# Hybrid retention and short-convolution block: seven-product groups with 512-wide matmuls, 40 input groups in that form, retention after them, and part sums made by an accumulating DMA

## Chip, cores and metric

One Trainium2 chip, one of its NeuronCores. The metric is the device time of one execution in microseconds (us), the median of several runs. Engines are named as in the profile: PE (matrix multiply), PEld (its weight loads), DVE (vector), ACT (scalar activation), POOL (which also issues DMAs), SP (which issues the weight loads from memory).

## What is computed

One encoder layer on 512 tokens of width 2048, in float32:

```python
h = rmsnorm(x, norm_gain)
proj = h @ w_in                       # 2048 x 12288
q, k, v, g_ret, c_b, c_c, c_x, g_conv, merge_logits = split(proj)
o = bidirectional_retention(rotary(q), rotary(k) * 128 ** -0.5, v)   # 8 heads of 128
branch_ret = o * rsqrt(mean(o * o) + EPS) * ret_gn_gain * silu(g_ret)
branch_conv = c_b * conv3(c_c * c_x) * silu(g_conv)
up = [branch_ret @ w_branch[0], branch_conv @ w_branch[1]]           # each 1024 x 2048
merged = sum(sigmoid(merge_logits) * up)
x = rmsnorm(x + merged @ w_out, final_gain)                          # 2048 x 2048
```

## The kernel before

Every float32 operand is split into a high and a low part in the PE's own format (`split_to`: ACT writes the high part, L140, DVE the remainder, L141). A product of two operands takes three matmuls (`mm3`, L145 to L147): high by high, high by low and low by high, all accumulated in one region of PSUM.

The work is a list of *pieces*, each of four k-tiles (128 rows) by 256 columns of a weight matrix. `run` keeps the loads of weights (SP's queue, L105, three buffers) three pieces ahead, the splits two ahead (three buffers for the high part, two for the low), calls the piece's matmuls, and then pops one entry of the list `background`. An order is only proposed in this way: a scheduler at build time fixes the order on each engine by its own estimates. On the chip each engine runs its instructions in that order and waits where an input is late. A DMA that POOL issues waits in POOL's queue for its inputs in the same way.

The input projection has 48 groups of 256 columns, four pieces each: 4 for each of q, k, v and the retention gate g, 16 for the convolution branch, 16 for the merge gates.

- `group` (L171) makes the eight 128-column by 512-token products of a piece (96 matmuls of 512 columns in a group). `group_tok` (L277, for v) puts tokens on the output's partitions: 192 matmuls of 256 columns.
- `group_s` (L197) replaces eight products of half blocks by seven, in the manner of Strassen and Winograd: the 2 x 2 blocks are two k-tiles by two column halves, and two k-tiles by two token halves of 256. Seven combinations of weight blocks (three of them summed on DVE in `sums`, L134 to L136) meet seven combinations of token blocks (`token_forms`, L263: sums and differences of h, made once per pair of k-tiles and kept in SBUF). `combine` (L247) adds the seven results with one copy on ACT (L253) and four additions on DVE (L255 to L260), reading PSUM. 27 groups go this way: 16 of the convolution, 11 of the merge gates.

Order: transposes of x and the first k group; for each of four pairs of heads the groups k, q, v, g, with the retention of that pair (`retention_steps`, L528: eight steps for two heads: decay table, scores, output, norm, store to memory by POOL) popped from `background` one step per piece; three plain gate groups, under which the token forms are made; the 27 seven-product groups; two plain gate groups, during which both branches are loaded back and split; the two up-projections, alternating by column group; the output projection with the final norm. Results that are needed later (gates, branch outputs) go to memory and come back by POOL's queue.

## Time and profile before

| | us |
|---|---|
| median of 3 runs | 1443.73 (1442.91 to 1446.1) |
| the profiled execution | 1444.66 |
| its span in the trace | 1442.8 |
| granted PE clock, mean | 0.995 of full speed |

The span runs from the first to the last event of the trace; the execution's own time has a little beside it. Busy time of PE is a union of overlapping records, so the price of a matmul is read from the distance between starts. "Idle before, releaser" says what ended an engine's wait. An engine off the limiting chain may be idle at no cost.

### The profile page before, as it was taken

How to read it: one execution, taken by the hardware profiler on the slowest of the kernel's cores; microseconds unless marked ns; L12 is line 12 of the kernel's file. 1: busy time of each engine (PE TensorE's matmuls, PEld its weight loads, DVE VectorE, ACT ScalarE, POOL GpSimd, SP SyncE). 2: the span in 40 equal slices, each digit the busy share in tenths (PEclk: the TensorE clock that was granted, in tenths of full speed). 3: DMA queues.
4: the chain of work that ended last, by engine and by line, in shares of the span. 5: the costliest groups of instructions: out<-in, count | busy, mean ns of one | idle time of the engine just before them, and what ended most of it. 6: DMA issues, size and time to landing. Idle time of an engine off the chain costs nothing.

```text
span 1442.8 us, 20988 instructions
## 1 busy us (share of the span) xinstructions
PE 1423.4 (99%) x8810; PEld 1286.1 (89%) x8810; DVE 945.2 (66%) x1220; ACT 549.2 (38%) x586; POOL 65.8 (5%) x80
## 2 busy tenths in 40 slices
PE   8999999999999999999999999999999999999997
PEld 7888988988988899999999999999978888888886
DVE  4846557466467989988898899889643444522433
ACT  6435335354344434443344334434342222222421
POOL 0000000000000000000000000000010000201210
PEclk9999999999999999999999999999999999999999
DMA  6322322322323333443344334433464444543412
GB/s 229 94 87 84 107 77 86 102 79 97 102 68 121 117 95 106 140 132 103 103 132 135 100 116 134 132 103 103 148 231 161 146 146 146 186 179 102 162 55 105
DMA packets 140610, 174.93 MB, mean 121 GB/s; under 512 B 5940, under 2 KB 122724, under 8 KB 139876
## 3 DMA queue, kind: packets, MB, share of 16 engines
q1 hardware_dynamic: 132788, 143.17, 30.7%
q0 software_dynamic: 7696, 30.41, 6.3%
q8 instruction: 69, 1.13, 0.3%
q14 instruction: 25, 0.20, 0.0%
q10 hardware_dynamic: 32, 0.01, 0.0%
HBM read 156.79 MB, written 16.78 MB: 120 GB/s over the span
## 4 chain that ended last, share of the span: by engine, by line
PE 92%; DVE 5%; DMA 2%; issue 1%; ACT 0%; SPq 0%; DVEq 0%; ACTq 0%
PE acc L147 29%; PE acc L145 29%; PE acc L146 29%; DVE wlo L141 2%; DMA raw<-in_w_in_dram 1%; PE op L147 1%; PE sp L147 1%; PE sp L145 1%; PE op L145 1%; PE op L146 1%; PE sp L146 1%; DVE raw L134 0%; PE xtp L346 0%; DMA xb<-in_x_dram 0%; DVE fl L141 0%
## 5 line engine op out<-in xcount | busy, mean ns | idle before, releaser
L141 DVE TENSOR_TENSOR wlo<-raw,whi 128x1024 fp32r<-128x1024 f32 (+2 forms) x257 | 402.5, 1568 | 351.0 <-PE acc L147 139.8
L140 ACT ACTIVATE whi<-raw 128x1024 fp32r<-128x1024 f32 (+2 forms) x257 | 339.6, 1326 | 560.1 <-PE acc L146 312.9
L147 PE MATMUL acc<-hTh,wlo 128*128 128x256 f32 (+1 forms) x1192 | 396.0, 332 | 2.4 <-DVE wlo L141 2.4
L145 PE MATMUL acc<-hTh,whi 128*128 128x256 f32 (+1 forms) x1192 | 396.6, 333 | 0.7 <-DVE de L257 0.7
L146 PE MATMUL acc<-hTl,whi 128*128 128x256 f32 (+1 forms) x1192 | 395.9, 332 | 0.0
L147 PEld LDWEIGHTS acc<-hTh,wlo 128*128 128x128 f32 x1192 | 227.0, 190 | 24.9 <-DVE wlo L141 3.3
L147 PE MATMUL acc<-fh,wlo 128*128 128x256 f32 x864 | 245.5, 284 | 2.6 <-DVE wlo L141 2.6
L145 PEld LDWEIGHTS acc<-hTh,whi 128*128 128x128 f32 x1192 | 227.2, 191 | 22.1 <-issue 0.8
L146 PEld LDWEIGHTS acc<-hTl,whi 128*128 128x128 f32 x1192 | 227.1, 191 | 21.2
L145 PE MATMUL acc<-fh,whi 128*128 128x256 f32 x864 | 244.6, 283 | 0.3 <-DVE T L574 0.2
L146 PE MATMUL acc<-fl,whi 128*128 128x256 f32 x864 | 244.5, 283 | 0.0
L147 PEld LDWEIGHTS acc<-fh,wlo 128*128 128x128 f32 x864 | 166.1, 192 | 3.6 <-DVE wlo L141 3.3
L145 PEld LDWEIGHTS acc<-fh,whi 128*128 128x128 f32 x864 | 166.0, 192 | 0.8 <-DVE T L574 0.4
L146 PEld LDWEIGHTS acc<-fl,whi 128*128 128x128 f32 x864 | 166.0, 192 | 0.0
L146 PE MATMUL acc<-wlo,mTh 128*128 128x512 f32 (+1 forms) x272 | 102.5, 377 | 0.0
L147 PE MATMUL acc<-whi,mTl 128*128 128x512 f32 (+1 forms) x272 | 102.5, 377 | 0.0
L145 PE MATMUL acc<-whi,mTh 128*128 128x512 f32 (+1 forms) x272 | 102.5, 377 | 0.0
L145 PE MATMUL acc<-bh,whi 128*128 128x512 f32 x256 | 99.6, 389 | 0.0
L146 PE MATMUL acc<-bl,whi 128*128 128x512 f32 x256 | 99.6, 389 | 0.0
L147 PE MATMUL acc<-bh,wlo 128*128 128x512 f32 x256 | 99.6, 389 | 0.0
L134 DVE TENSOR_TENSOR raw<-raw 128x512 f32<-128x512 f32 x108 | 74.3, 688 | 16.4 <-DMA raw<-in_w_in_dram 16.3
L146 PE MATMUL acc<-wlo,hTh 128*128 128x256 f32 x256 | 72.4, 283 | 0.0
(171 smaller groups left out, 1546.0 us busy)
## 6 DMA issues: line engine op xcount, KB each, us to landing
raw<-in_w_in_dram SPq DMA_DIRECT2D x191, 512.0 KB, 3.6
raw<-in_w_branch_dram SPq DMA_DIRECT2D x32, 512.0 KB, 3.3
raw<-in_w_out_dram SPq DMA_DIRECT2D x32, 512.0 KB, 3.6
gate_d<-T POOLq DMA_DIRECT2D x16, 512.0 KB, 3.8
gl<-gate_d POOLq DMA_DIRECT2D x16, 512.0 KB, 4.4
y<-in_x_dram POOLq DMA_DIRECT2D x4, 1024.0 KB, 6.6
xb<-in_x_dram SPq DMA_DIRECT2D x12, 256.0 KB, 6.4
ret_d<-tmp POOLq DMA_DIRECT2D x8, 256.0 KB, 2.4
```

Source lines behind the costliest of these rows:

```text
L134: nc.vector.tensor_tensor(s[:, 0:2].rearrange("p f r x -> p r f x"), diag, b21, op=ALU.add)
L140: pin(nc.scalar.activation(hi, src, AF.Copy))
L141: pin(nc.vector.tensor_tensor(lo, src, hi.bitcast(F32), op=ALU.subtract))
L145: pin(nc.tensor.matmul(acc, lh, rh, start=start, stop=False, **kw))
L146: pin(nc.tensor.matmul(acc, lh, rl, start=False, stop=False, **kw))
L147: pin(nc.tensor.matmul(acc, ll, rh, start=False, stop=stop, **kw))
```

## The change

1. In `group_s` the high weight now meets both token parts in one 512-wide matmul, into both halves of a PSUM bank; the low weight meets the high token part in a 256-wide matmul, added into the second half. Seven tiles of one bank each (eight in the pool) replace four banks by two pools. Blocks pair k-tile j with k-tile j + 8.
2. ACT copies each product from PSUM to one SBUF buffer `ev` (one slot) in the group's last piece. `sum_parts` then adds the second halves to the first by an accumulating DMA on POOL's queue, and by a second one adds the product named m1 to two of the sums. `combine` makes the remaining three additions on DVE from SBUF.
3. 40 groups use this form: q, g, all 16 gates and the 16 of the convolution. k (4) and v (4) stay plain. h lies in three tiles, so that for half of the k-tiles a k matmul is cut in two of 256 columns. The token forms are made in the background of the k and the first two v groups.
4. Rotated k and q, v and g go to memory. Retention runs as 22 background entries under the conv up-projection and the last two v groups, from operands that POOL loads back and that are split again; then the ret up-projection follows by itself. A quarter of h is written to memory and read back for those v groups.
5. Pools are re-laid: weights get new buffers after the seven-product stage, in the space of the token forms.

The diff, cut to its core:

```diff
+    big = ctx.enter_context(tc.tile_pool(name="big", bufs=1))
+    tpp = ctx.enter_context(tc.tile_pool(name="tp", bufs=3, reuse_waits="tile"))
...
+        nc.vector.tensor_tensor(s[:, 0:2].rearrange("p f r x -> p r f x"), diag, both21, op=ALU.add)
+        nc.vector.tensor_tensor(b21, s[:, 1], b22, op=ALU.add)
+        nc.vector.tensor_tensor(s[:, 2], b21, b12, op=ALU.add)
...
-                        mm3(
-                            st["acc"][:, j, :],
-                            (wh[:, k, c], wl[:, k, c]),
-                            (rhs()[0][:, kt, :], rhs()[1][:, kt, :]),
-                            kt == 0,
-                            kt == nk - 1,
-                        )
+                        for t, r in rhs(kt):
+                            mm3(
+                                st["acc"][:, j, t : t + r.shape[2]],
+                                (wh[:, k, c], wl[:, k, c]),
+                                (r[:, 0], r[:, 1]),
+                                kt == 0,
+                                kt == nk - 1,
+                                skip_group_check=True,
+                            )
...
-                    pool = ps if state["banks"] % 2 == 0 else fin["psS"]
+                    tiles = [fin["p7"].tile([P, 2, 256], F32, name="acc", tag="acc") for _ in order]
+                    st["acc"] = tiles if state["banks"] else [tiles[i] for i in (4, 5, 6, 2, 3, 0, 1)]
                     state["banks"] += 1
-                    st["acc"] = [pool.tile([P, 2, S], F32, name="acc", tag="acc") for _ in range(2)]
-                for n, (bank, half, b, a) in enumerate(order):
-                    acc = st["acc"][bank // 2][:, bank % 2, half * 256 : half * 256 + 256]
+                for n, (b, a, place) in enumerate(order):
+                    acc = st["acc"][n]
                     for r in range(2):
-                        mm3(
-                            acc,
-                            [weight_form(w, b, r) for w in pc["w"]],
-                            token_form(a, 2 * q + r),
-                            q == 0 and r == 0 and n in seen,
-                            q == KT // 4 - 1 and r == 1,
-                            skip_group_check=True,
-                        )
+                        wh, wl = [weight_form(w, b, r) for w in pc["w"]]
+                        x = token_form(a, q + 4 * r)
+                        first, last = q == 0 and r == 0, q == KT // 4 - 1 and r == 1
+                        nc.tensor.matmul(acc, wh, x, start=first, stop=False, skip_group_check=True)
+                        nc.tensor.matmul(acc[:, 1, :], wl, x[:, 0], start=False, stop=last, skip_group_check=True)
+                    if q == KT // 4 - 1:
+                        nc.scalar.activation(EV()[:, :, place, :], acc, AF.Copy)
                 if q == KT // 4 - 1:
-                    post(combine(*st["acc"]))
-            pieces.append({"dims": (4, 256), "src": src[:, 4 * q : 4 * q + 4, :], "use": use, "forms": True})
+                    sum_parts()
+                    if pc.get("defer"):
+                        state["defer"] = lambda: post(combine())
+                    else:
+                        post(combine())
+            rows = src.rearrange("p (i q) c -> p i q c", q=4)[:, :, q, :]
+            pieces.append({"dims": (4, 256), "src": rows, "use": use, "forms": True})
+
+    def EV():
+
+        return fin["ev"]
+
+    def sum_parts():
+        e = EV()
+        nc.gpsimd.dma_start(out=e[:, 0, 0:7, :], in_=e[:, 1, 0:7, :], accum_op=ALU.add)
+        m1 = e[:, 0, 6:7, :].broadcast_to([P, 2, 256])
+        nc.gpsimd.dma_start(out=e[:, 0, 4:6, :], in_=m1, accum_op=ALU.add)
...
-    def combine(x, y):
-
-        tp = part["tp"]
-        t = tp.tile([P, 2, S], F32, name="T", tag="T", bufs=3)
...
+    def combine():
+
+        e = EV()[:, 0]
+        t = T()
         flat = t.rearrange("p j (i s) -> p (j i) s", i=2)
-        s = tp.tile([P, S], F32, name="sc", tag="sc", bufs=1)
-        nc.scalar.activation(s, x[:, 0, :], AF.Copy)
-        halves = lambda v: v.rearrange("p (i s) -> p i s", i=2)
-        nc.vector.tensor_tensor(flat[:, 1:3, :], halves(s), halves(x[:, 1, :]), op=ALU.add)
-        d = tp.tile([P, S], F32, name="de", tag="de", bufs=1)
-        nc.vector.tensor_tensor(halves(d), halves(s), swapped(x[:, 1, :]), op=ALU.subtract)
-        m1 = y[:, 0, 0:256].unsqueeze(1).broadcast_to([P, 2, 256])
-        nc.vector.tensor_tensor(halves(d), halves(d), m1, op=ALU.add)
-        nc.vector.tensor_tensor(flat[:, 0:4:3, :], halves(d), halves(y[:, 1, :]), op=ALU.add)
+        s, back = e[:, 0:2, :], e[:, 3, :]
+        back = bass.AP(back.tensor, back.offset, [back.ap[0], [-256, 2], [1, 256]])
+        nc.vector.tensor_tensor(flat[:, 1:3, :], s, e[:, 2:4, :], op=ALU.add)
+        nc.vector.tensor_tensor(s, s, back, op=ALU.subtract)
+        nc.vector.tensor_tensor(flat[:, 0:4:3, :], s, e[:, 4:6, :], op=ALU.add)
         return t
...
+    def h_rows(kt):
+
+        if kt < 8:
+            return [(0, h1[:, :, kt, :])]
+        return [(0, h_part(kt, 0)), (256, h_part(kt, 256))]
...
+    def retention_program():
+
         L = lambda f, *v: (lambda: f(*v))
-        return [
-            [L(decay_table, a), L(score, a, 0), L(score, a, 1)],
...
+        n = 22
+        return [sum(steps[k * len(steps) // n : (k + 1) * len(steps) // n], []) for k in range(n)]
...
+    others = [(cols(0, i), rotary_post(q_d, i)) for i in range(4)] + [(cols(3 * BW, i), g_post(i)) for i in range(4)]
+    others += [(cols(8 * BW, i), gate_post(i)) for i in list(range(8, 16)) + list(range(8))]
...
     for i in range(BW // 256):
+        for n, (off, post) in enumerate(conv_posts(i)):
+            group_s(cols((4 + off) * BW, i), post)
+            for _ in range((1, 2, 1, 2)[n]):
+                group_s(*others.pop(0))
+    assert not others
+    pieces[-1]["defer"] = True
...
+    for n in range(2):
+        up_group(1, n, conv_up_post(n))
+    for i in range(2, 4):
+        group_tok(cols(2 * BW, i), v_post(i))
+        up_group(1, i, conv_up_post(i))
+    for i in range(4, 8):
+        up_group(1, i, conv_up_post(i))
+    n_r = len(pieces)
     for i in range(D // 256):
-        for n in range(2):
-            c = slice(i * 256, (i + 1) * 256)
-            group(wb[n][:, :, c], BW // P, lambda n=n: brs[n], up_post(n, i))
+        up_group(0, i, ret_up_post(i))
...
+    for j in range(KT // 2):
+        background.extend([[lambda j=j: token_forms(j)], []])
+    run(n_a)
     while background:
+        for f in background.pop(0):
+            f()
+    psx.close()
+    h10x.close()
+    with tc.tile_pool(name="p7", bufs=8, space=PSUM) as p7:
+        fin["p7"] = p7
+        lr = ctx.enter_context(tc.tile_pool(name="lr", bufs=1, reuse_waits="tile"))
+        fin["ev"] = lr.tile([P, 2, 7, 256], F32, name="ev", tag="h10", padded_shape=[P, 2, 8, 256])
+        run(n_s)
+    fms.close()
+    hx.close()
+
+    pools["ps"] = ctx.enter_context(tc.tile_pool(name="psR", bufs=2, space=PSUM))
+    pools["wp"] = ctx.enter_context(tc.tile_pool(name="wpR", bufs=3, reuse_waits="tile"))
+    pools["WF"] = 1024
+    bbx = ExitStack()
+    bb = bbx.enter_context(tc.tile_pool(name="bb", bufs=1, reuse_waits="tile"))
+    bt = [bb.tile([P, 2, 2, S], F32R, name=f"b{i}") for i in range(4)]
+
+    brs[1] = lambda kt: [(0, bt[kt // 2][:, :, kt % 2, :])]
+    state["limit"] = len(pieces)
+    for _ in range(3):
+        load(pieces[state["loaded"]])
+        state["loaded"] += 1
+    for i in range(4):
+        load_branch(1, i)
+    split_upto(n_s + 2)
+    state["defer"]()
...
+    fetch(0)
+    fetch_head(0)
+    background.extend(retention_program())
+    run(n_r - 2)
+    while background:
+        for f in background.pop(0):
+            f()
+    br0 = rps["br0"] = big.tile([P, 2, GG, S], F32R, name="br0", tag="h1")
+    brs[0] = lambda kt: [(0, br0[:, :, kt, :])]
+    rps["stg"] = big.tile([P, 2, 2, 2, S], F32, name="stg", tag="h00")
+    for i in range(2):
+        load_merge(i)
+    for i in range(4):
+        load_branch(0, i)
+    run(n_r)
...
```

## Rows read from the trace of the kernel before

**Rows 1.** The page: busy time by engine (part 1), the chain by engine (part 4).
```profile
PE 1423.4 (99%) x8810; PEld 1286.1 (89%) x8810; DVE 945.2 (66%) x1220; ACT 549.2 (38%) x586; POOL 65.8 (5%) x80
...
PE 92%; DVE 5%; DMA 2%; issue 1%; ACT 0%; SPq 0%; DVEq 0%; ACTq 0%
```
**Rows 2.** Busy time of each engine in windows (start:end and length in us).
```profile
core 0: us, PE busy (x) PEld busy (x) DVE busy (x) ACT busy (x) POOL busy (x), PEclk, DMA share, GB/s
64.00:464.00 400.00, 400.00 (x2115) 345.40 (x2114) 232.31 (x309) 175.95 (x218) 5.25 (x9) 1.00 0.29 91
464.00:500.00 36.00, 33.79 (x188) 29.11 (x186) 34.72 (x46) 15.91 (x13) 1.44 (x2) 1.00 0.32 103
500.00:504.00 4.00, 3.92 (x20) 3.93 (x21) 3.63 (x6) 0.35 (x1) 0.00 (x0) 0.57 0.58 171
500.00:1036.50 536.50, 535.74 (x4445) 535.21 (x4446) 470.84 (x578) 211.23 (x155) 9.99 (x14) 1.00 0.38 119
1036.50:1080.00 43.50, 40.42 (x178) 32.76 (x177) 23.55 (x22) 18.41 (x18) 8.53 (x12) 1.00 0.62 206
```
**Rows 3.** Timeline of PE, seven-product stage: first and last of 70 matmuls (start, length).
```profile
699.79 0.28 PE L146 MATMUL acc<-hTl,whi 128*128 128x256 f32 x1
...
708.07 0.28 PE L146 MATMUL acc<-fl,whi 128*128 128x256 f32 x1
```
**Rows 4.** Timeline of PE, plain part: first and last of 13 matmuls.
```profile
160.03 0.39 PE L147 MATMUL acc<-hTh,wlo 128*128 128x512 f32 x1
...
162.75 0.39 PE L147 MATMUL acc<-hTh,wlo 128*128 128x512 f32 x1
```
**Rows 5.** Groups by line and shape, PE (one line of three): count, busy us, mean ns.
```profile
L145 PE MATMUL acc<-fh,whi 128*128 128x256 f32 x864 | 244.6, 283 | 0.3 <-DVE T L574 0.2
...
L145 PE MATMUL acc<-hTh,whi 128*128 128x512 f32 x544 | 212.8, 391 | 0.7 <-DVE de L257 0.7
...
L145 PE MATMUL acc<-hTh,whi 128*128 128x256 f32 x648 | 183.9, 284 | 0.0
...
L145 PE MATMUL acc<-bh,whi 128*128 128x512 f32 x256 | 99.6, 389 | 0.0
```
**Rows 6.** Timeline of PE: the last stop ahead of the seven-product stage.
```profile
500.07 0.39 PE L147 MATMUL acc<-fh,wlo 128*128 128x256 f32 x1 [1.38 <-DVE wlo L141]
...
500.71 0.42 PE L145 MATMUL acc<-hTh,whi 128*128 128x256 f32 x1
500.92 0.42 PE L146 MATMUL acc<-hTl,whi 128*128 128x256 f32 x1
```
**Rows 7.** Groups by line and shape: DVE and ACT in the seven-product stage.
```profile
L141 DVE TENSOR_TENSOR wlo<-raw,whi 128x1792 fp32r<-128x1792 f32 x108 | 218.0, 2022 | 32.0 <-PE acc L147 24.6 <-ACT whi L140 6.8
...
L140 ACT ACTIVATE whi<-raw 128x1792 fp32r<-128x1792 f32 x108 | 182.5, 1700 | 186.4 <-DVE raw L136 110.4 <-PE acc L146 63.2 <-PE acc L147 12.9
...
L259 DVE TENSOR_TENSOR de<-de,acc 128x512 f32<-128x512 f32 x27 | 18.4, 681 | 0.0
...
L253 ACT ACTIVATE sc<-acc 128x512 f32<-128x512 f32 x27 | 15.9, 589 | 29.9 <-PE acc L147 29.9
L574 DVE TENSOR_TENSOR T<-T,rsrow 128x1024 f32<-128x1024 f32 x11 | 13.4, 1221 | 0.0
```
**Rows 8.** The page, DMA issues (part 6): count, KB each, us from issue to landing.
```profile
gate_d<-T POOLq DMA_DIRECT2D x16, 512.0 KB, 3.8
...
y<-in_x_dram POOLq DMA_DIRECT2D x4, 1024.0 KB, 6.6
...
ret_d<-tmp POOLq DMA_DIRECT2D x8, 256.0 KB, 2.4
...
bl<-ret_d POOLq DMA_DIRECT2D x4, 512.0 KB, 5.8
```
**Rows 9.** Groups by line and shape: DVE in the retention.
```profile
L481 DVE SCALAR_TENSOR_TENSOR tmp<-sp,tb 128x512 f32<-128x512 f32 x32 | 21.2, 686 | 6.8 <-PE sp L147 6.8
...
L469 DVE SCALAR_TENSOR_TENSOR tb<-dist,lg,tb 128x896 f32<-128x896 f32 x8 | 9.2, 1145 | 0.0
```

More of the change, by code (lines that the diff above doesn't have):

```diff
@@ L151, in split_upto @@
     def split_upto(n):
-        while state["split"] < min(n, len(pieces)):
+        while state["split"] < min(n, state["limit"]):
             split(pieces[state["split"]])
@@ L158, in run @@
             i = state["used"]
-            while state["loaded"] < min(i + 4, len(pieces)):
+            while state["loaded"] < min(i + 4, state["limit"]):
                 load(pieces[state["loaded"]])
@@ L414, in hybrid_block_kernel, with both, pair, rotary_post @@
     heads = {}
-    def rotary_post(name, h0):
+    def both(row):
+        return row.unsqueeze(1).broadcast_to([P, 2, S])
+    def pair(d, i):
+        return d[2 * i : 2 * i + 2].rearrange("d p s -> p d s")
+    def rotary_post(d, i):
         def post(acc):
@@ L432, in rotary_post, with v_post @@
+            r = T() if acc.tensor.name.startswith("acc") else acc
+            nc.scalar.activation(sw[0:64], acc[64:128], AF.Copy)
+            nc.scalar.activation(sw[64:128], acc[0:64], AF.Copy)
+            nc.vector.tensor_tensor(r, acc, both(rot[:, 0, :]), op=ALU.mult)
+            nc.vector.tensor_tensor(sw, sw, both(rot[:, 1, :]), op=ALU.mult)
+            nc.vector.tensor_tensor(r, r, sw, op=ALU.add)
+            nc.gpsimd.dma_start(out=pair(d, i), in_=r)
         return post
-    def v_post(h0):
+    def v_post(i):
@@ new lines, in fetch_head, with split_head @@
+    def fetch_head(h):
+        hd = heads.setdefault(h, {})
+        for n, d in (("k", k_d), ("q", q_d)):
+            hd[n + "f"] = rps["sb"].tile([P, S], F32, name="st", tag="st", bufs=3)
+            nc.gpsimd.dma_start(out=hd[n + "f"], in_=d[h])
+    def split_head(h):
+        hd = heads[h]
+        for n in ("k", "q"):
+            hi = rps["sb"].tile([P, S], F32R, name=n + "h")
+            lo = rps["sb"].tile([P, S], F32R, name=n + "l")
+            split_to(hi, lo, hd[n + "f"])
+            hd[n] = (hi, lo)
@@ new lines, in load_merge, with ret_up_post, post @@
+    def load_merge(i):
+        nc.gpsimd.dma_start(out=slot(0, i), in_=pair(gate_d[0], i))
+        nc.gpsimd.dma_start(out=slot(1, i), in_=pair(m1_d, i))
+    def ret_up_post(i):
+        def post(acc):
+            t = slot(0, i)
+            nc.vector.tensor_tensor(t, acc, t, op=ALU.mult)
+            nc.vector.tensor_tensor(t, t, slot(1, i), op=ALU.add)
+            k = slice(2 * i, 2 * i + 2)
+            split_to(mT[0][:, k, :], mT[1][:, k, :], t)
+            if i + 2 < D // 256:
+                load_merge(i + 2)
+        return post
@@ L801, in hybrid_block_kernel @@
     square_x(XC - 1)
-    ps_x.__exit__(None, None, None)
-    xst.close()
-    rps["p"] = ret.enter_context(tc.tile_pool(name="rps", bufs=2, space=PSUM))
-    rps["sb"] = ret.enter_context(tc.tile_pool(name="ret", bufs=2, reuse_waits="tile"))
     run(XC)
@@ L812, in hybrid_block_kernel @@
     log_decays()
-    run(n_ret)
-    while background:
-        if state["used"] < n_fill:
-            run(state["used"] + 1)
-        else:
-            for f in background.pop(0):
-                f()
-    ret.close()
-    with tc.tile_pool(name="fm", bufs=1, reuse_waits="tile") as fm:
-        part["forms"] = [fm.tile([P, KT // 2, 4, 256], F32R, name=n) for n in ("fh", "fl")]
-        background.extend([[lambda j=j: token_forms(j)] for j in range(KT // 2)])
-        while background:
-            if state["used"] < n_fill:
-                run(state["used"] + 1)
-            else:
-                for f in background.pop(0):
-                    f()
-        run(n_fill)
-        with tc.tile_pool(name="psS", bufs=2, space=PSUM) as psS:
-            fin["psS"] = psS
-            run(n_s)
@@ L846, in hybrid_block_kernel @@
-    mT.append(big.tile([P, KT, S], F32R, name="mTl", tag="big"))
+    ps_x.__exit__(None, None, None)
+    xst.close()
+    for z in range(2):
+        nc.gpsimd.dma_start(out=a21_d[z].rearrange("j p s -> p j s"), in_=hold["h10"][:, z])
+    fms = ExitStack()
+    fm = [
+        fms.enter_context(tc.tile_pool(name=f"fm{i}", bufs=1, side="right", reuse_waits="tile")).tile(
+            [P, 2, 2, 4, 256], F32R, name="fm"
+        )
+        for i in (3, 2, 1, 0)
+    ]
+    part["forms"] = fm[::-1]
@@ new lines, in hybrid_block_kernel @@
+    for _ in range(3):
[5 more added lines that the diff above has]
+    state["defer"]()
+    rsx.close()
+    hold["h10"] = lr.tile([P, 2, KT // 2, 256], F32R, name="h10", tag="h10")
+    for z in range(2):
+        nc.gpsimd.dma_start(out=hold["h10"][:, z], in_=a21_d[z].rearrange("j p s -> p j s"))
+    ret = ExitStack()
+    rps["sb"] = ret.enter_context(tc.tile_pool(name="ret", bufs=2, side="right", reuse_waits="tile"))
```

391 lines of the change are left out of this document (190 added, 201 removed).

## Prediction

> **What bounds it now.** Read first the page's busy shares and chain: TensorE (PE) is busy for 99% of the span and makes 92% of the chain of waits; no other engine passes 66% [rows 1]. So the time is PE's own issue time plus its few stops. The windows by stage say where those are: none in 64 to 464 us, 2.2 us in 464 to 500, 0.8 us in the seven-product stage (500 to 1036.5), 3.1 us behind it. VectorE (DVE) is busy for 470.84 of that stage's 536.5 us, 88%: the second limit [rows 2].
>
> Then the price of one matmul, as the distance between starts, since records overlap. In the seven-product stage 70 matmuls of 256 columns start between 699.79 and 708.07: 8.28/69 = 0.1200 us each [rows 3]. In the plain part 13 of 512 columns start between 160.03 and 162.75: 2.72/12 = 0.2267 [rows 4]. At 2.4 GHz that is 288 and 544 cycles: the columns plus 32 either way. So 32 cycles (13.3 ns) are paid per instruction, and a 512-wide one pays them once for twice the columns.
>
> **The sum on PE.** Before, a seven-product group is 4 pieces x 7 products x 2 k-tiles x 3 = 168 matmuls of 256: 20.16 us. 27 such groups give the 864 + 648 matmuls on each of the three lines [rows 5]. A plain group is 96 of 512: 21.76 us. After, each product and k-tile takes one 512-wide matmul (high weight against both token parts) and one of 256: 56 x (0.2267 + 0.1200) = 19.41 us.
> - 27 groups that already use seven products: 27 x (19.41 - 20.16) = -20.2 us.
> - 13 groups (q, g and the five plain gates) go from eight products to seven: 13 x (19.41 - 21.76) = -30.5 us.
> - The four k groups: half of h now lies in two 256-wide pieces, so 48 of 512 and 96 of 256 instead of 96 of 512: 4 x (22.40 - 21.76) = +2.6 us.
> - v, both up-projections, retention and the output keep their matmuls: 0.
>
> Check by counts: 800 more of 512, 1912 fewer of 256, 181.4 - 229.4 = **-48.1 us**. An alternation of 512 and 256 is in no long row; both widths pay the same 32 cycles and adjoin in the trace without a stop, so I add the two. Bounds for the pair: 0.3467 us, or no better than the three 256-wide matmuls it replaces, 0.360 (then 2240 x 0.0133 = 30 us of the gain are gone).
>
> The Trainium skill ("TensorE: Matmul & The Clock Gate", Back-to-back issue gap) gives N/2.4 + 2.5 ns per matmul: 215.8 and 109.2 ns here. By it an instruction saved is worth less, and the same counts give 172.6 - 208.8 = -36.2 us, an estimate. The trace disagrees (226.7 and 120.0), so the rows decide.
>
> **What else is moved.**
> - *Token forms.* Before, they are squeezed in right before the seven-product stage, DVE 34.72 of 36 us busy, and PE stops [rows 2]. After the last stop, 1.38 us, PE's starts lie 0.21 us apart and the granted clock of 500 to 504 is 0.57, the 1.2 GHz level for most of it; 20 matmuls start where 33 would, a loss that includes a little of the stop [rows 2, 6]. After, the forms run one in every second of 24 plain pieces with no retention beside them: about 4 us of DVE per 11 us, beside 2 x 1.2 us of weight split. Covered. I take -2.0 us of stops and -1.5 us of slow clock: **-3.5 us**. If that cover fails, the same stop stays.
> - *DVE in the seven-product stage.* Now 470.84 us in 26.6 groups (536.5/20.16) = 17.7 us a group. The weight sums and splits stay (the split of 1792 elements is the largest part [rows 7]); of four combining additions three stay (-0.68 [rows 7]); the finishing work stays near 2.2 us (11 gates of 1.22 and four conv units over 27 groups, then 16 gates, four q of three such operations, four g and the same units over 40). So 17.1 of 19.41 us, 88% again: DVE doesn't become the bound by load, with 2.3 us spare per group.
> - *ACT in it.* Four splits of 1.70 us, seven evictions of 0.59 where one stood, and about 1.2: 12.1 of 19.41 us, hidden [rows 7].
> - *The sums by DMA.* Per group POOL issues an accumulate of 128 x 7 KB (896 KB), then one of 256 KB that waits for the first, then the store; POOL's queue is in order, so a late store also holds the next accumulates. DVE's combine waits for them. Behind it on DVE stand the weight splits of the next pieces, on which PE waits. The next group's evictions must not overwrite the one buffer before combine has read it, and behind those on ACT stand splits too. No accumulating DMA is in this trace. Nearest rows, from issue to landing: 256 KB 2.4 us, 512 KB 3.8, 1024 KB 6.6 [rows 8]; by line between them 896 KB is 5.9. Lower end 5.9 + 2.4 = 8.3 us, if an accumulate costs a copy. Upper end: source and destination are both read, so 1792 and 512 KB: 6.6 + 768 x 2.8/512 = 10.8, plus 3.8 = 14.6 us. The buffer's circle is evictions 6 x 0.69 + 0.59 = 4.8, the DMAs, and the last combining addition 0.7: 13.8 to 20.1 us, before any wait in DVE's queue, against a period of 19.41. I take a value near the copy, the row of the same sizes, with some missed slots: **+6 us** over the stage; ends 0 and the second rival below.
> - *Retention* moves behind, into 22 of 24 pieces of the conv up-projection and the last v groups. PE there: 16 x 24 x 0.2267 + 8 x 48 x 0.12 + 208 x 0.2267 = 87.0 + 46.1 + 47.2 = 180 us, work that only changes place. DVE: per head eight score operations of 0.69 [rows 9], some ten more of that shape and 1.8 for the decay table [rows 9], 8 x 14.2 = 114 us, plus 36 splits and gates of 1.22 = 44: 158 of 180 us by records, against 58% where retention runs now [rows 2]. Before, that stage has no stop; at this density I take **+4 us** (0 to 25). In its last pieces the last head runs norm, store (2.4), reload (5.8) and split (2.3) [rows 7, 8] behind about 7 us of its own chain, 17.5 us, under two pieces and what of the ret up-projection goes first, 17.7: **+1 us** (0 to 6).
> - *Stage borders.* Behind the seven products 3.1 us are lost now; the new pools reuse the forms' space piece by piece, and the first branch tiles are split while the last piece runs. 0, from -3 to +3. SP issues only weight loads there, three ahead as before.
>
> Sum: -48.1 - 3.5 + 6 + 4 + 1 = -40.6. The profiled execution took 1444.66 us (span 1442.8), so 1404; the median of the runs is 0.9 us lower: **1403 us**.
>
> **The rivals.**
> 1. *The accumulate circle, slower than before.* Place: the eviction buffer with one slot in 40 groups. At the upper end, 20.1 us, plus up to one weight split of 2.0 us that DVE has begun when the sum lands, 22.1 us: 0.7 to 2.7 us over the period, 28 to 108 us in 40 groups, in place of my 6: up to 1397 + 108 = 1505, and more if waits slow the clock. It decides from 1.2 us over the period, that is from DMAs of about 13 us together with that split, 15 without. For: nothing here shows an accumulate, and weight loads use 0.38 of the DMA engines already [rows 2]. Against: the copies of these sizes leave 3.7 us to spare. The Trainium skill ("Collectives: The Full Stack", The bandwidth ceiling: the fold count and why AG ≠ RS ≠ AR) says an adding DMA needs two source reads and so runs at half of a copy's rate; no row here shows it.
> 2. *DVE's order.* The circle fits, but the instruction order is fixed when the kernel is built, and DVE stands at combine while splits are due. Spare are 2.3 us a group; waits of 2.8 to 3.4 cost 0.5 to 1.1 us x 40 = 20 to 44 us: 1417 to 1441. For: DVE is the releaser of nearly all of PE's stops now.
> 3. *Retention too dense.* Its 158 us of DVE work in chains through ACT and PE keep it from running ahead: 10 to 25 us in place of my 4, 1409 to 1424.
> 4. *The pair costs 0.360.* The change then saves only through 13 groups: 1403 + 30 = 1433.
>
> **How the numbers follow.** Forecast as summed 0.52 (own range 1390 to 1416); rival 1, 0.19; rival 2, 0.17; rival 3, 0.08; rival 4, 0.04. A measurement tells about 0.2% (2.9 us) from no change. Rivals 2 (but for 0.04 at its upper end), 3 and 4 are still faster: faster 0.77, same 0.04, slower 0.19. The range runs from the sum without any new stall and 3 us off the borders, 1444 - 48 - 3.5 - 3 = 1389, up to 1446, which leaves out rival 1 alone.
>
> **What would show it.** Right: 8,810 - 1,112 = 7,698 matmuls; starts 0.347 us apart per pair; a seven-product group every 19.4 us, the stage near 777 us; PE waiting for DVE by a few us in all. Wrong: accumulates from issue to landing above 13 us together, ACT waiting for combine before evictions, or DVE idle before the first combining addition for over 2.3 us a group; clock rows below 1.00 in that stage; PE idle on score or output tiles in the retention stage.

## The result, and the profile after

After the change the kernel takes **1617.16 us** (median of 4 runs, 1614.84 to 1620.5), before it 1443.38 (4 runs): a ratio of 1.1201, 95% interval 1.1177 to 1.1226. 1403 was forecast, so the change is 174 us slower where it should have been 40 faster. The profiled execution took 1617.48 us, its span is 1615.7.

The page of the kernel after: busy time, four of the rows in 40 slices, POOL's software DMA queue, and the chain by engine and by line.

```profile
PE 1454.3 (90%) x7698; PEld 1244.7 (77%) x7698; DVE 1060.5 (66%) x1372; ACT 700.8 (43%) x828; POOL 191.9 (12%) x224
...
PE   9999888889888898888888888887899999999997
...
DVE  4875777777768768657677677676578875542433
...
PEclk9999999899999999899999999999899999999999
DMA  8433466566565565555656655657854655563422
...
q0 software_dynamic: 35600, 106.97, 27.6%
...
PE 26%; DMA 16%; issue 12%; DVE 12%; ACT 5%; POOL 1%; DVEq 0%; ACTq 0%; POOLq 0%
DMA ev<-ev 13%; PE acc L166 7%; PE acc L165 7%; PE acc L167 7%; DVE wlo L161 5%; PE acc L244 3%; PE acc L245 2%; ACT ev L247 2%; ACT whi L160 2%; DMA raw<-in_w_in_dram 1%; DMA st<-q_d 1%; DVE raw L154 1%; POOL ev L263 1%; DMA T<-conv_d 0%; DVE raw L155 0%
```

There are the forecast 7,698 matmuls, but PE, which made 92% of the chain [rows 1], makes 26% of it now, and the accumulating DMAs (`ev<-ev`) 13%. The windows by stage say where the time is lost (columns as in [rows 2]; the rows are the end of the plain part, the seven-product stage, its border behind, the part with the retention, and the part behind that):

```profile
64.00:154.00 90.00, 88.34 (x675) 84.27 (x674) 60.73 (x83) 34.43 (x37) 3.26 (x5) 1.00 0.36 118
152.70:1137.50 984.80, 851.10 (x4480) 727.53 (x4480) 694.73 (x832) 445.64 (x479) 102.80 (x108) 0.93 0.59 149
1137.50:1172.00 34.50, 27.48 (x107) 21.29 (x105) 16.99 (x17) 12.45 (x14) 12.53 (x17) 0.90 0.97 270
1172.00:1330.00 158.00, 154.07 (x831) 132.40 (x832) 129.90 (x182) 94.61 (x125) 30.14 (x48) 0.98 0.55 184
1330.00:1450.00 120.00, 117.80 (x511) 96.62 (x510) 60.10 (x54) 34.37 (x34) 20.11 (x23) 0.99 0.59 200
```

The seven-product stage (second row) takes 984.8 us, 24.62 a group, where 19.41 were forecast: 208 of the 214 us of the miss. PE stands still for 133.7 us of it, and is busy for 851.10 at a granted clock of 0.93; the same 4,480 matmuls take it 781.57 us in the first experiment below. The other stages lose little. The list of waits names what ends the stops (us in total, times, longest):

```profile
ACT whi L160 <- DVE raw L156: 317.3, 78, 11.2
...
PE acc L245 <- DVE wlo L161: 131.7, 51, 5.7
DVE T L288 <- DMA ev<-ev: 124.2, 34, 5.5
...
DVE T L290 <- DMA ev<-ev: 65.4, 36, 5.7
...
DVE raw L154 <- DMA raw<-in_w_in_dram: 57.5, 43, 5.9
...
ACT ev L247 <- PE acc L245: 27.7, 20, 6.9
```

PE waits for the low part of the weights, which DVE makes. DVE, in its turn, waits at combine's first addition (L288) for the first accumulate and at its third (L290) for the second, 189.6 us or 4.7 a group, and for weight tiles from memory (57.5 us). The evictions (ACT's copies from PSUM into `ev`, last row) wait for PE and never for combine: the circle through the one buffer doesn't bind.

In the order of DVE's instructions, fixed when the kernel is built, combine's first addition stands behind the third 1792-wide split of the next group in 38 of 39 groups; what is behind it waits with it. From issue to landing (page, last column) the accumulates take 7.9 and 3.8 us, and the weight loads beside them 4.2:

```profile
raw<-in_w_in_dram SPq DMA_DIRECT2D x191, 512.0 KB, 4.2
ev<-ev POOLq DMA_DIRECT2D x40, 896.0 KB, 7.9
...
ev<-ev POOLq DMA_DIRECT2D x40, 256.0 KB, 3.8
```

### The profile page after: what moved, and what is told of

Its sections match the earlier page's. It is cut to its first block, busy times and chain, and to the rows that moved or that the text cites. A ratio compares the mean times of both kernels' runs of the same rounds, so it can differ in the third digit from the quotient of the medians.

```text
span 1615.7 us, 19583 instructions
## 1 busy us (share of the span) xinstructions
PE 1454.3 (90%) x7698; PEld 1244.7 (77%) x7698; DVE 1060.5 (66%) x1372; ACT 700.8 (43%) x828; POOL 191.9 (12%) x224
## 4 chain that ended last, share of the span: by engine, by line
PE 26%; DMA 16%; issue 12%; DVE 12%; ACT 5%; POOL 1%; DVEq 0%; ACTq 0%; POOLq 0%
DMA ev<-ev 13%; PE acc L166 7%; PE acc L165 7%; PE acc L167 7%; DVE wlo L161 5%; PE acc L244 3%; PE acc L245 2%; ACT ev L247 2%; ACT whi L160 2%; DMA raw<-in_w_in_dram 1%; DMA st<-q_d 1%; DVE raw L154 1%; POOL ev L263 1%; DMA T<-conv_d 0%; DVE raw L155 0%
## 5 line engine op out<-in xcount | busy, mean ns | idle before, releaser
L160 ACT ACTIVATE whi<-raw 128x1792 fp32r<-128x1792 f32 (+2 forms) x257 | 373.3, 1459 | 590.7 <-DVE raw L156 317.3
L161 DVE TENSOR_TENSOR wlo<-raw,whi 128x1792 fp32r<-128x1792 f32 (+2 forms) x257 | 440.3, 1716 | 183.9 <-PE acc L166 59.0
L245 PE MATMUL acc<-fm,wlo 128*128 128x256 f32 x1280 | 369.5, 289 | 131.7 <-DVE wlo L161 131.7
L244 PE MATMUL acc<-fm,whi 128*128 128x512 f32 x1280 | 464.1, 401 | 2.6 <-ACT T L483 1.7
L244 PE MATMUL acc<-h,whi 128*128 128x512 f32 x960 | 383.3, 430 | 1.0 <-ACT ev L247 1.0
L245 PEld LDWEIGHTS acc<-fm,wlo 128*128 128x128 f32 x1280 | 247.1, 193 | 149.8 <-DVE wlo L161 149.6
L244 PEld LDWEIGHTS acc<-fm,whi 128*128 128x128 f32 x1280 | 245.4, 192 | 58.0 <-ACT T L483 1.9
L245 PE MATMUL acc<-h,wlo 128*128 128x256 f32 x960 | 287.3, 300 | 0.0
L244 PEld LDWEIGHTS acc<-h,whi 128*128 128x128 f32 x960 | 201.7, 210 | 50.6 <-ACT ev L247 1.5
L154 DVE TENSOR_TENSOR raw<-raw 128x512 f32<-128x512 f32 x160 | 109.7, 686 | 57.9 <-DMA raw<-in_w_in_dram 57.5
L288 DVE TENSOR_TENSOR T<-ev 128x512 f32<-128x512 f32 x40 | 27.6, 691 | 124.2 <-DMA ev<-ev 124.2
L165 PE MATMUL acc<-whi,mT 128*128 128x512 f32 (+1 forms) x272 | 103.0, 379 | 0.0
L167 PE MATMUL acc<-whi,mT 128*128 128x512 f32 (+1 forms) x272 | 102.1, 375 | 0.0
L290 DVE TENSOR_TENSOR T<-ev 128x512 f32<-128x512 f32 x40 | 27.6, 691 | 65.4 <-DMA ev<-ev 65.4
```

Of the source, the lines that this page charges most:

```text
L154: nc.vector.tensor_tensor(s[:, 0:2].rearrange("p f r x -> p r f x"), diag, both21, op=ALU.add)
L160: pin(nc.scalar.activation(hi, src, AF.Copy))
L161: pin(nc.vector.tensor_tensor(lo, src, hi.bitcast(F32), op=ALU.subtract))
L165: pin(nc.tensor.matmul(acc, lh, rh, start=start, stop=False, **kw))
L167: pin(nc.tensor.matmul(acc, ll, rh, start=False, stop=stop, **kw))
L244: nc.tensor.matmul(acc, wh, x, start=first, stop=False, skip_group_check=True)
```

## The experiments

These rows allow three theories. **A**: DVE stands at combine until the sums land, and the splits behind it come late for PE. **B**: the accumulates' traffic delays the weight loads, whoever waits for the sums. **C**: the circle through the eviction buffer binds. A rival, **D**, is that the loss doesn't come from the DMAs at all. Raw tiles are the three buffers in which weight loads land; high tiles hold the high part of the split weights. Waits are totals of a whole run. Every run stands beside one of the kernel before on the same chip (1441.9 to 1444.4 us), and is one timed execution where no interval is given.

### 1. No sums at all

```diff
 def sum_parts():
+    return
```
(both accumulates are left out)

> Leaves out both accumulating DMAs (the part sums and m1 are not added). The changed kernel needs 24.6 us per seven-product group, 205 us more over 40 groups than the 19.41 of PE's own work. Theory A (DVE stands at combine until the accumulates land): all of that goes, a group near 19.5 us, the time about 1410 us (1400 to 1425). Theory B (the accumulates' traffic delays the weight loads): the same, about 1410. Theory C (the circle through the one eviction buffer): the same. Rival D (the losses are not the DMAs': mixed matmul widths, DVE's own load, evictions on ACT): the group stays above 22 us, the time above 1510.

1411.51 us. The seven-product stage, in a window:

```profile
154.20:939.10 784.90, 781.57 (x4480) 681.84 (x4480) 695.01 (x832) 444.39 (x480) 22.06 (x31) 1.00 0.41 129
```
784.9 us, 19.62 a group, at full clock; DVE works as much as with the sums (695.01 and 694.73). So 206 us hang on two DMAs in 40 groups, rival D is out, and the rest of the change does about what was forecast. DVE's wait for weight tiles and the landing of the loads are the base for the runs below:

```profile
DVE raw L154 <- DMA raw<-in_w_in_dram: 38.3, 32, 3.8
...
raw<-in_w_in_dram SPq DMA_DIRECT2D x191, 512.0 KB, 3.8
```

### 2. The sums made, and nobody waiting for them

```diff
-    nc.gpsimd.dma_start(out=e[:, 0, 0:7, :], in_=e[:, 1, 0:7, :], accum_op=ALU.add)
+    nc.gpsimd.dma_start(out=e[:, 1, 0:7, :], in_=e[:, 0, 0:7, :], accum_op=ALU.add)
```
(the second likewise, inside the second halves; combine reads the first halves only)

> Both accumulates run with the same sizes and order, but into the second halves, and combine reads only the first halves, so nothing on DVE waits for them (the sums are left out of the result); the next evictions still wait for them. Theory A: the group falls to 19.5 to 20 us, the time to 1410 to 1435. Theory B: weight loads are as late as before, DVE waits for them, the time stays above 1530. Theory C: the circle loses only the combining part; evictions 4.8 + DMAs with issue 13.8 = 18.6 us, so near A, 1410 to 1450, with ACT seen waiting before evictions.

1507.94 us, 96 above the run without sums, with no wait at combine. That lies between theory A's forecast (1435 at most) and theory B's (above 1530), so neither is the whole. What DVE waits for is now the weight tiles, 154.3 us where it was 38.3 without sums:

```profile
DVE raw L154 <- DMA raw<-in_w_in_dram: 154.3, 79, 6.1
...
PE acc L245 <- DVE wlo L161: 54.5, 39, 3.8
```

One place in its timelines (start, length; POOL, SP and DVE) shows how:

```profile
702.80 0.87 POOL L263 DMA_DIRECT2D ev<-ev  x1 [17.30 <-ACT ev L247]
...
710.59 1.19 POOL L265 DMA_DIRECT2D ev<-ev  x1 [3.81 <-DMA ev<-ev]
```
```profile
703.57 0.37 SPq L125 DMA_DIRECT2D raw<-in_w_in_dram  x1
...
711.62 0.69 DVE L154 TENSOR_TENSOR raw<-raw 128x512 f32<-128x512 f32 x1 [3.53 <-DMA raw<-in_w_in_dram]
```
The first accumulate is issued at 702.80 and has landed by 710.59, when the second goes out. A weight load issued 0.77 us behind it lands only at 711.6, 8.0 us after its issue where 3.8 are usual (the median without sums), and DVE idles 3.53 us for it. It isn't a single case: of the 126 loads issued between 150 and 1150 us, 62 went out while an accumulate was under way, and their median is 7.6 us; that of the others is 4.0. In 702.8 to 710.5 all DMA engines together move 162 GB/s at a busy share of 0.84. The Trainium skill ("DMA: Bandwidth & Descriptors", Issuing engines are not separate DMA queues) says that transfers from the scalar, sync and GpSimd queues run on the same 16 engines and interleave; the trace agrees (8.0 us in place of 3.8, at that share of 0.84).

### 3. Combine behind the third piece, by the order of the program alone

```diff
-                        post(combine())
+                        state["late"] = lambda: post(combine())
+                elif q == 2 and state.get("late"):
+                    state.pop("late")()
```


> The whole computation; combine and the finishing work of a group are emitted after the third piece of the next group instead of behind the last piece of its own, so that DVE has splits to do while the accumulates run. Theory A: DVE waits little at combine, 1410 to 1460. Theory B: above 1530. Theory C: the buffer is held longer, evictions wait for it: 1600 or more.

1612.61 us, and nothing learned about the theories: the scheduler put combine back to the same place in DVE's order (behind the third split of the next group, in 39 of 39), and DVE still waits 89.3 and 78.7 us at it. Number 6 holds it in place.

### 4. Three 256-wide matmuls, no sums needed

```diff
-    nc.tensor.matmul(acc, wh, x, start=first, stop=False, skip_group_check=True)
-    nc.tensor.matmul(acc[:, 1, :], wl, x[:, 0], start=False, stop=last, skip_group_check=True)
+    mm3(acc[:, 0, :], (wh, wl), (x[:, 0], x[:, 1]), first, last, skip_group_check=True)
```
(one half evicted, the product m1 added on DVE)

> The 512-wide matmul undone: three 256-wide matmuls per product into one half, no accumulates, m1 added on DVE (one more addition of 0.6 us); 40 groups and retention behind stay. PE needs 20.16 us a group, DVE 17.7. Theories A, B and C: 19.41 -> 20.16 in 40 groups is +30 us on the run without sums, about 1440 (1430 to 1455), so the rest of the change is worth about nothing against the kernel before. Rival D: above 1510.

1431.42 us, at the lower end of what was expected: 20 us above the run without sums, where 30 were forecast. It is 13 us under the kernel before (one execution of each), where about nothing was expected: the change without its 512-wide matmul and without the DMAs is worth having.

### 5. The first accumulate alone

```diff
-        nc.gpsimd.dma_start(out=e[:, 0, 4:6, :], in_=m1, accum_op=ALU.add)
...
+        nc.vector.tensor_tensor(s, s, e[:, 6:7, :].broadcast_to([P, 2, 256]), op=ALU.add)
```


> The second accumulate (256 KB, which waits for the first) is left out; DVE adds the same product in its own third addition, three combining additions plus one of 0.7 us again. The first accumulate of 896 KB stays, and so do the places of the combining additions in DVE's order. Theory A (DVE stands at combine until the sums land): the chain ends 3.8 us earlier plus one issue of 1.2 us; DVE's waits at combine, 189.6 us with the change, fall to about the part of the first sum's, some 60 to 120 us, and the time to 1500 to 1550 us. Theory B (the accumulates' traffic delays the weight loads): 896 of 1152 KB stay, so some 96 x 0.78 = 75 us of loss by traffic stay, and the wait of the split for the raw tile stays at 60 us or more; 1490 us is the floor. Theory C (circle through the eviction buffer): 4.8 + 7.9 + 2 us is under the period, and the loss would go: about 1420.

1543.15 us: 74 us back. DVE's waits at combine fall from 189.6 to 124.1 us, while the wait for weight tiles stays (54.4 us, 57.5 with the change). That is near theory A's forecast; by C the time would have been 1420, so C is out.

### 6. Combine held one piece later

```diff
+                elif q == 1 and state.get("late"):
+                    state.pop("late")()
...
+        if not state.get("defer"):
+            tc.keep_in_program_order(ins)
```


> Both accumulates stay; the combining additions are held behind the second piece of the next group, one 1792-wide split later in DVE's order than with the change (about 5 us). The sums have landed 13 to 15 us after the last product; one more piece gives about 5 to 6 us. Theory A: DVE's waits at combine (189.6 us) fall below 60 us; by A alone the time falls by about as much as they do, to 1480 to 1530. Theory B: the loads stay as slow as with the change, the wait for the raw tile rises to 100 us or more, as in the run whose sums nobody waits for, and the time doesn't fall below that run's 1508. Theory C: combine later lengthens the circle by 5 us, and the scalar engine's evictions wait for it: no better than 1617, or worse.

1527.85 us, 89 back, at the upper end of A. DVE's waits:

```profile
DVE raw L154 <- DMA raw<-in_w_in_dram: 110.7, 70, 4.4
...
DVE T L294 <- DMA ev<-ev: 60.5, 24, 4.2
...
DVE T L290 <- DMA ev<-ev: 7.5, 10, 1.0
```
Those at combine (L290 and L294) are 68.0 us together, a little over the 60 of the forecast; that for weight tiles has risen from 57.5 to 110.7. As expected by A and B together, the time ends near that of the run whose sums nobody waits for.

### 7. Plain copies in place of the accumulates

```diff
-        nc.gpsimd.dma_start(out=e[:, 0, 0:7, :], in_=e[:, 1, 0:7, :], accum_op=ALU.add)
+        nc.gpsimd.dma_start(out=e[:, 0, 0:7, :], in_=e[:, 1, 0:7, :])
```
(the second likewise)

> Both accumulates become plain copies of the same source, target and order; the sums are then left out of the computation (the copy overwrites the first half). Everything else, the waits of combine too, stays. If an accumulate costs a plain copy, as the prediction took it: the time stays within 10 us of 1617 and the landing at 7.9 and 3.8 us. If adding makes it dearer (twice the reads): landing falls to about 5.9 and 2.4 us, the DMA share in 520 to 900 from about 0.6 to about 0.5, and the time to 1500 to 1580. Theory A gives 40 x (7.9 + 3.8 - 8.3) = 136 us as the most that the landing alone can give back.

1477.71 us, less than either forecast, for the two copies together land sooner than was assumed (7.8 us in place of 8.3):

```profile
ev<-ev POOLq DMA_DIRECT2D x40, 896.0 KB, 4.9
...
ev<-ev POOLq DMA_DIRECT2D x40, 256.0 KB, 2.9
```
That is 7.8 us together against 11.7. So an accumulate costs 1.6 times a copy of 896 KB and 1.3 times one of 256 KB, not the same, and that is 139 us of the time (both ways of loss together: DVE's waits at combine are down to 77.1 us). But copies, which land within the prediction's lower price (8.3 us), still cost 66 us over no DMAs, not 0 to 6: the landing was not the only error.

### 8. The sums on POOL

```diff
-        nc.gpsimd.dma_start(out=e[:, 0, 0:7, :], in_=e[:, 1, 0:7, :], accum_op=ALU.add)
+        nc.gpsimd.tensor_tensor(e[:, 0, 0:7, :], e[:, 0, 0:7, :], e[:, 1, 0:7, :], op=ALU.add)
```
(the second likewise; combine held as in 6)

> GpSimd adds both sums itself (two additions per group in its idle time) where it issued the accumulates; combine is held behind the second piece of the next group. No accumulating traffic at all. GpSimd's addition of 512 elements took 1.63 us before, so about 5.7 us for 1792 and 1.7 for 512, 7.4 us per group. Theories A and B both give back nearly all of the loss: 1410 to 1430 us, no slower raw loads (3.8 us), DMA share about 0.4. If GpSimd's additions slow DVE's (both work in the same memory), DVE at 88% becomes the bound: splits of 1.8 us get longer and the time is 1430 to 1500.

1566.56 us, dearer than expected, and for another reason. DMA share is down to 0.35, weight loads land in 3.9 us; but DVE needs longer for less: in 520 to 900 it is busy for 351.47 of 380 us with 340 instructions, where without sums it did 404 in 335.74. POOL's timeline, then DVE's:

```profile
703.89 4.07 POOL L265 TENSOR_TENSOR ev<-ev 128x1792 f32<-128x1792 f32 x1 [2.54 <-ACT ev L247]
708.04 1.62 POOL L267 TENSOR_TENSOR ev<-ev 128x512 f32<-128x512 f32 x1
```
```profile
705.03 3.48 DVE L154 TENSOR_TENSOR raw<-raw 128x512 f32<-128x512 f32 x1 [0.99 <-DMA raw<-in_w_in_dram]
708.54 1.40 DVE L155 TENSOR_TENSOR raw<-raw 128x256 f32<-128x256 f32 x1
709.98 0.42 DVE L156 TENSOR_TENSOR raw<-raw 128x256 f32<-128x256 f32 x1
```
An addition that takes DVE 0.69 us takes 3.48, and ends half a microsecond behind POOL's (707.96); the next takes 1.40 in place of 0.42. Over the run the first of these additions (L154) takes 1.17 us on average, 0.69 without sums. The Trainium skill ("SBUF — State Buffer", Who interferes with whom) says that a DVE instruction with two SBUF inputs contends with a GpSimd instruction that reads SBUF, and the trace agrees (3.48 us in place of 0.69).

### 9 and 10. A fourth weight tile

```diff
-name="raw", tag="raw", bufs=3)
+name="raw", tag="raw", bufs=3 if "WF" in pools else 4)
...
-fl.append(pools["wp"].tile([P, pools.get("WF", WF)], F32R, name=n, tag=n, bufs=k))
+fl.append(pools["wp"].tile([P, pools.get("WF", WF)], F32R, name=n, tag=n, bufs=k if "WF" in pools else 2))
```
(and loads one piece further ahead; number 9 as number 2, number 10 as number 1)

> As the run with both accumulates that nobody waits for (1507.9 us), with four raw weight tiles in place of three, loads issued one piece further ahead, and two tiles of high weights in place of three to make room. Theory B in this form: the accumulate fills the DMA engines for some 12 us a group, a 512 KB weight load issued under it lands 8 us after its issue in place of 3.8, and with three tiles the load is issued too late to bear that. Then one more tile (5 us more of lead per load) takes most of it away: DVE's wait for raw tiles, 143.2 us, falls below 40 us, and the time to 1420 to 1445 us. If the traffic costs in another way (the engines' access to memory, a clock that falls by itself): the waits for raw tiles fall and the time stays above 1480 us. If two high tiles are what costs, the control without the sums shows it.

> The control: no accumulates and no sums (1411.5 us with three raw tiles), four raw tiles and two of high weights. If the third high tile is of no use here: 1405 to 1413 us. If it is: more, and the run with the accumulates is read against this one.

Number 9 took 1474.14 us and number 10 1411.16. The control is unharmed. With the accumulates, 34 of the 96 us came back, which is neither forecast (DVE's wait below 40 us, or a time above 1480): DVE still waits 132.6 us for weight tiles. ACT, with two high tiles, now stands at the split for PE (281.4 us), but it does so in the control too (223.3), at no cost. The fourth raw tile was paid for with the third high one, so this is no clean test of depth, and why a fourth tile gives so little stays open. Where the 96 us come from is settled by number 13.

### 11. Both remedies

Number 6 with the four tiles of number 9.

> The whole change, correct sums by both accumulates, with both remedies: combine held behind the second piece of the next group (1527.9 us alone) and four raw tiles. Theories A and B together, as two costs that add up: DVE's wait at combine stays near 60 us, of the rest most goes, 1440 to 1480 us. If B was what kept combine's chain late too (its stores and loads in the same queues), down to 1425. If the raw tiles are not the place of B: 1500 to 1530.

1509.29 us, 67 us above the kernel before and worse than the 1440 to 1480 forecast for two costs that add up; it lies in the range named for the case that the raw tiles are not the place of B. DVE hardly waits for the sums any more (6.7 us, at L294), but 156.3 us for weight tiles, and with combine this late the circle does begin to bind: ACT's evictions wait 74.7 us for combine's last addition. So four tiles don't cure B here, as in number 9; that B comes about through the loads rests on numbers 2 and 13.

### 13 and 14. No weight loads in the stage

The first three pieces' tiles are used for all 160; sums, splits and products stay.

```diff
+        if pc.get("forms") and len(kept) >= 3:
+            pc["F"] = kept.pop(0)
+            kept.append(pc["F"])
...
+            return
```


> Both accumulates at work, nobody waiting for them (1507.9 us), and in the seven-product stage no weight loads: its first three pieces are loaded and the 157 others use those three tiles again, so that the products are of wrong weights; every sum, split, product and eviction stays. Theory B by the loads: nothing is left for the accumulates to delay; the stage is PE's own 785 us again and the time 1405 to 1415 us. If the traffic slows the engines themselves (longer splits, sums, evictions) or the clock falls by itself: 1440 us or more, with longer instructions or a clock row below 1.00 where PE doesn't stop.

1415.36 us: with both accumulates at work, but no load for them to delay, the 96 us are gone but for 4. The whole stage, and 520 to 900 us of it:

```profile
155.06:933.75 778.69, 778.69 (x4479) 681.47 (x4480) 700.30 (x829) 444.95 (x476) 103.34 (x109) 1.00 0.39 83
...
520.00:900.00 380.00, 380.00 (x2188) 332.57 (x2187) 339.69 (x403) 217.56 (x236) 49.74 (x52) 1.00 0.37 78
```
There is no stop and full clock, and the instructions are no longer than without sums (a 1792-wide split takes DVE 2.02 us in both; in number 2 as well). **B is shown, and its way is the weight loads.** 2188 matmuls in 380 us are 380 x 112/2188 = 19.45 us a group, the forecast's 19.41.

> The change as it is, with combine's waits for the sums, and without the weight loads of that stage, as in the run before. Theory A alone remains: if the two costs add up, 1617 - 96 = 1520 us; if the loads that come late in the same stretch account for part of what DVE's waits seem to cost (a late load behind a late combine), below 1500; if the accumulates land sooner with the DMA engines to themselves (5.9 in place of 7.9 us), 1450 to 1480. DVE's wait at combine was 189.6 us.

1534.18 us, with DVE's waits at combine still there:

```profile
DVE T L296 <- DMA ev<-ev: 94.2, 36, 5.7
...
PE acc L253 <- DVE wlo L169: 78.8, 43, 4.9
...
DVE T L298 <- DMA ev<-ev: 64.9, 40, 5.6
...
154.17:1055.92 901.75, 822.94 (x4479) 707.59 (x4480) 694.84 (x829) 451.10 (x480) 103.53 (x109) 0.96 0.33 72
...
ev<-ev POOLq DMA_DIRECT2D x40, 896.0 KB, 6.4
```
The window is that of the stage, the last line the landing of the first accumulate. So A alone costs 1534 - 1415 = 119 us, B alone 1508 - 1412 = 96; together 215, against 206 measured: the two nearly add up. The 896 KB land in 6.4 us without weight loads in the stage, in 7.9 beside them, so A's share beside the loads isn't measured by itself.

### 12 and 15. Two or three products as pairs, their parts added on DVE

Five products as in number 4, two as pairs whose parts DVE adds (number 15: four and three). No DMA takes part in the sums, and DVE adds m1 as in number 4.

```diff
+                        if place < 2:
+                            nc.tensor.matmul(acc, wh, x, start=first, stop=False, skip_group_check=True)
+                            nc.tensor.matmul(acc[:, 1, :], wl, x[:, 0], start=False, stop=last, skip_group_check=True)
+                        else:
+                            mm3(acc[:, 0, :], (wh, wl), (x[:, 0], x[:, 1]), first, last, skip_group_check=True)
...
+        nc.vector.tensor_tensor(e[:, 0, 0:2, :], e[:, 0, 0:2, :], e[:, 1, 0:2, :], op=ALU.add)
```


> A version without accumulating DMAs: five of the seven products as three 256-wide matmuls into one part (as in the run at 1431.4 us), two products as the pair of 512 and 256, their two parts added on DVE (one addition of 512 elements, 0.69 us a group; the m1 addition on DVE too). PE: 2 x 8 x 0.0133 = 0.21 us less per group, 8.5 us in 40 groups; DVE: about 18.8 of 19.9 us. If DVE still has the room: 1421 to 1425 us. If DVE becomes the bound at some 94%: 1425 to 1440, no better than three everywhere.

1426.84 us (4 runs), 0.9898 of the kernel before, interval 0.9882 to 0.9915: 15 us faster, though 2 us above the best case that was expected (1421 to 1425). It is only 4.6 us under number 4, whose one execution stands at 0.9910 of the kernel before on its own chip, inside this interval: that the pairs add to number 4 isn't shown clear of noise. PE has no stop in the middle of the stage, and DVE is at 91%:

```profile
520.00:900.00 380.00, 380.00 (x2903) 365.96 (x2902) 346.47 (x433) 192.49 (x228) 9.31 (x13) 1.00 0.40 124
```

> As the version with two pairs (1426.8 us), three products as pairs, their parts added on DVE (one addition of 768 elements, about 0.95 us). PE: 0.107 us less per group, 4.3 us in 40: 1422.5 if DVE (91% busy with two) still has the room; 1425 to 1432 if it doesn't.

1434.52 us (4 runs), 0.9948, interval 0.9932 to 0.9965: still faster than before, but 8 us slower than with two. In the same window:

```profile
520.00:900.00 380.00, 379.78 (x2736) 357.42 (x2736) 351.90 (x433) 193.12 (x225) 9.28 (x13) 1.00 0.39 124
```
DVE is at 93%, and a group takes 380 x 144/2736 = 20.00 us, not the 19.84 of its matmuls. That DVE became the limit was expected in this case, but it isn't shown: PE, too, is busy for 379.78 of the 380 us, and what was late was not followed up.

## Why the prediction was wrong

Point by point, by its steps:

- **The sum on PE: right.** The count is 7,698, and a pair starts every 0.345 us, as its timeline shows (start, length):

```profile
155.59 0.39 PE L244 MATMUL acc<-fm,whi 128*128 128x512 f32 x1
155.82 0.28 PE L245 MATMUL acc<-fm,wlo 128*128 128x256 f32 x1
155.93 0.40 PE L244 MATMUL acc<-fm,whi 128*128 128x512 f32 x1
156.17 0.28 PE L245 MATMUL acc<-fm,wlo 128*128 128x256 f32 x1
156.28 0.39 PE L244 MATMUL acc<-fm,whi 128*128 128x512 f32 x1
```

  Rival 4 (0.360) is out, and 512 and 256 may be added from their separate rows.
- **DVE and ACT by load: near.** 17.1 and 12.1 us a group were forecast; without sums they are 695.01/40 = 17.4 and 444.39/40 = 11.1.
- **Token forms, retention, borders: near.** In the windows after, PE is idle for 1.7 us ahead of the stage, 7.0 behind it where 3.1 were lost [rows 2] (the forecast was no change), 3.9 under the retention (forecast 4) and 2.2 behind that (forecast 1). Rival 3 is out. For all but the sums together, number 1 has 1411.5 against 1398, the prediction's 1404 for a profiled execution less its 6 for the sums; 8.5 of these 13 us are the stage's 784.9 against 40 x 19.41.
- **The sums by DMA: the step that failed.** It read "I take a value near the copy, the row of the same sizes, with some missed slots: **+6 us** over the stage". What was set at 6 us measured 206. Three things were wrong in it. *The price*: 11.7 us from issue to landing, not 8.3; it lay inside the bounds of 8.3 to 14.6, and nearly in their middle (11.45). *The wait*: rival 2 had the mechanism, DVE standing at combine with splits behind it, but allowed it 20 to 44 us and a chance of 0.17. It costs some 119 (number 14): there the waits are 159.1 us, 4.0 a group (4.7 with the change as it is), where 2.8 to 3.4 were set against 2.3 to spare, and PE, having stopped, works at a lower granted clock, 0.96, and is busy for 822.94 us with what takes 778.69 at 1.00 in number 13. *What the traffic does to others*: it was no term at all. That the loads use 0.38 of the DMA engines stood under rival 1 as a reason why accumulates might be late; that the accumulates would make the loads late was not asked. That is 96 us (numbers 2 and 13), and by itself enough to turn the gain into a loss.
- **Rival 1**, the only one that forecast a slower kernel, named the wrong place: evictions don't wait for combine until combine is moved (number 11). Its price, up to 1505 and more with a slower clock, was too low as well. Of the signs that the prediction gave for being wrong, DVE idle before combine's first addition (124.2/40 = 3.1 us a group) and the clock below 1.00 came true; a landing above 13 us and evictions that wait for combine did not.

With the waits at their price, but no delayed loads, the same sum gives 1398 + 119 = 1517, with the delayed loads alone 1398 + 96 = 1494. Neither could have been read from the trace before to a few microseconds. That the risk was larger than a chance of 0.19 for slower is argued, not shown: only 2.3 us a group were to spare, and 1152 KB of new transfers a group stood beside 2048 KB of loads that have three tiles.

## What to carry to other kernels

A DMA has two prices: what its reader waits for, and what it does to the transfers beside it; ask of each load that shares the engines how late it may come, and how many buffers stand behind that answer. Where a wait is put into a queue with a fixed order, price what stands behind it, not the wait; moving one addition by one split was worth 89 us here. And try the cheap half of an idea first: seven products in 40 groups paid off (13 us, number 4), while what two wide pairs add to that (4.6 us) isn't clear of noise, and a third pair cost 8 us against two.

## What the runs showed of the hardware that was not expected

- An accumulating DMA from SBUF to SBUF took 7.9 us for 896 KB beside the weight loads and 3.8 for 256, copies of the same shape 4.9 and 2.9. The Trainium skill ("Collectives: The Full Stack", The bandwidth ceiling: the fold count and why AG ≠ RS ≠ AR) puts the adding step of ReduceScatter, which needs two source reads, at half of AllGather's copying; that is a statement on collectives among cores, which no run here tests. For these accumulates inside one core's SBUF the time is 1.6 times a copy's for the large one and 1.3 times for the small one, not twice.
- Weight loads issued while such a transfer was under way landed 7.6 us after their issue (median of 62 in number 2), the others 4.0; the one shown landed 1.3 us after the accumulate.
- While POOL added, a DVE addition of two SBUF operands ended only after POOL's had: 3.48 us for 0.69 in the place shown, 1.17 on average over number 8.
